# Moving one projection pair ahead of v's stage, sending v's summed weights in one unit of two, and giving the last head one unit less before its products

## The chip, the cores and the metric

The kernel runs on one core of a Trainium2 chip. The metric is device time in microseconds (us) of one execution; the runs shown are three executions of the same program. A profile was taken of a further execution. Its records name the engines PE (TensorE, matmul), PEld (TensorE's load of the stationary operand), DVE (VectorE), ACT (ScalarE), POOL (GpSimd) and SP (the engine that starts most loads). A q behind a name is that engine's sequencer, which issues DMAs.

## What is computed

One decoder layer with two parallel groups, for 512 tokens of width 2048, in float32:

```
h = rmsnorm(x) * g_pre
q, k, v, z_att, u, g_glu, z_conv = split(h @ w_in)          # seven blocks of 1024 columns
# group A: 8 heads of 128, strictly causal stick-breaking attention
z     = q @ k.T / sqrt(128)
log_a = log_sigmoid(z) + (sum of -softplus(z) over the later keys before the query)
y_att = (where(causal, exp(log_a), 0) @ v) * silu(z_att)
# group B: gated, causal depthwise convolution of 31 taps, layer norm, swish, pointwise product
c      = layernorm(conv31(u * sigmoid(g_glu)) + conv_b)
y_conv = (silu(c) @ w_pw2 + b_pw2) * silu(z_conv)
out = x + rmsnorm(concat(y_att, y_conv) @ w_out) * g_post
```

## The kernel before

Every product is made of three matmuls: each operand is split into a rounded upper part (ScalarE, line 104) and the remainder (VectorE, line 105), and hi*hi, lo*hi and hi*lo are accumulated in PSUM (lines 351 to 353; in v's stage 661 to 663). A weight block of 1 MB is loaded by SP into one of two buffers `raw`, split into one of two `hi` and one of two `lo` buffers, and then used.

The work after the input norm is a list of **steps**. A step has one weight block and two **units**; a unit is the matmuls of one PSUM tile, 24 in a projection pair, 12 in v's stage. A `pair` makes 256 columns of a projection in two steps (the two halves of the 2048 rows). The steps are, in order: u pair 0 (`conv_in(0)`), q and k of heads 0 and 1 (`heads(0)`), a g pair (`gate_in(2)`), v's stage (`values()`, seven products `V_ORDER` of two steps each, a scheme with seven instead of eight block products), u pair 1 (`conv_in(1)`), heads 2 and 3, and so on through the other u, q, k and g pairs to the z_att pairs; behind them come z_conv, the pointwise product and the output product. `n_v` and `n_att` are the numbers of v's first step and of the first step behind v's stage, 8 and 22; `n_norm` is 48.

TensorE's order is the order written in the program. The order on VectorE, ScalarE and GpSimd is chosen at compile time by a list scheduler that goes by priorities; each engine then works through its own queue in order. The main loop over the steps (it starts near line 1427) issues beside each unit:

- **v's sums.** Four of v's seven products use weights that are sums of two blocks of `w_in`. The sums are made in device memory by GpSimd's DMA queue, a plain copy (line 528) and an accumulating copy (line 524) per block, 1 MB each, sixteen in all; tiles `vs`. Six are sent during the norm, the other ten one at a time by `sum_next(v_sumq)`, each not before the last matmul of the unit at hand. Products 5, 6, 7 and 4 of `V_ORDER = (1, 2, 5, 6, 3, 7, 4)` use them.
- **the other sums** (`sumq`, tiles `zs` and `ws`), from step 20 on, three in two steps.
- **attention.** `attention()` is a generator, advanced once per unit (`ticks` counts the units). It takes a head when its q and k are there and v's stage is over (`2 * n_att + 1`). For each head it issues the score products (`z`), lets four units pass (`SOFTMAX_TICKS`), issues the transposition of the weights (`aT`, line 742) and their split into `ah` and `al`, lets two units pass (`SPLIT_TICKS`), and issues the products with v (`o_ps`). During the four units ScalarE, VectorE and GpSimd make the weights; GpSimd masks them (line 698). Counted in units, heads 0 to 5 start at 45, 51, 57, 63, 69 and 75, heads 6 and 7 at 84 and 90; head 7's `aT` is at 94 and its `o_ps` at 96, the last unit before `n_norm`.
- **the convolution in the background.** Behind each u pair's second half, `post_u` multiplies the PSUM tile by the gate into `hg` (line 402; its 30 leading zeros are a GpSimd memset, line 401, and there are two `hg` buffers) and queues 32 entries per channel tile: 31 taps on VectorE (lines 405 and 410, tile `acc`) and one addition on GpSimd (line 424 or 426, `ln_sum`). `background` takes four entries after each unit, but one per unit in v's stage, and there the entry is tied behind the newest split of v's weights (`weights_split`). Its entries have a lower priority (`LATER`).

In v's stage VectorE also makes the sums of activations that the seven products need (`make_v_form`, lines 579 to 585) and their splits, and finishes v (`v_done`).

```
            if units_done % 4:
                sum_next(v_sumq)
...
                if n_v <= n < n_att:
                    background(1, LATER, weights_split[0])
                else:
                    background(4, LATER)
```

Of the kernel before, what the change touches and what calls it, by code (L numbers as in the profile page):

```python
# [23 lines left out]
NH = 8  # L24
# [16 lines left out]
SOFTMAX_TICKS, SPLIT_TICKS = 4, 2  # L41
# [12 lines left out]
def hybrid_layer(  # L54
# [127 lines left out]
    def turn_vectors():  # L182
        ps = mm("vec_ps")
        for c in range(CT):
            nc.tensor.transpose(
                ps[:, c * NV : (c + 1) * NV], rows[c // 4][:, c % 4 * P : (c % 4 + 1) * P],
                ident[:NV, :NV],
            )
        nc.vector.tensor_copy(
            vec, ps[:, : CT * NV].rearrange("p (c v) -> p c v", v=NV)  # L190
        )
# [166 lines left out]
    def pair(c0, post, name):  # L358

        ps = {}  # L360

        def unit(half, i):
            def go(w):
                hi, lo = w
                if half == 0:
                    ps[i] = mm(f"{name}_{i}")
                cs = slice(i * P, (i + 1) * P)
                for n in range(8):

                    k = n if c0 != C_U else (n + 4) % 8  # L370
                    mm3(
                        ps[i], (hi[:, k, cs], lo[:, k, cs]), h_at(half * 8 + k),
                        half == 0 and n == 0, half == 1 and n == 7,
                    )
                if half == 1:
                    post(i, ps[i])
            return go

        for half in range(2):
            src = w_in[half * 1024 : (half + 1) * 1024, c0 : c0 + 256]  # L380
            steps.append(Step(
                lambda src=src, half=half: stream(src, 8, f"{name}{half}"),
                [unit(half, 0), unit(half, 1)],
            ))
# [6 lines left out]
    def post_g(c):  # L391
        def post(i, ps):
            sig[c + i] = t2(f"sig{c + i}")
            nc.scalar.activation(sig[c + i], ps, AF.Sigmoid)
        return post

    def post_u(c):
        def post(i, ps):
            ct = c + i
            hg = hgp.tile([P, TAPS - 1 + S], F32, tag="hg", name=f"hg{ct}")  # L400
            nc.gpsimd.memset(hg[:, : TAPS - 1], 0.0)
            nc.vector.tensor_tensor(out=hg[:, TAPS - 1 :], in0=ps, in1=sig.pop(ct), op=ALU.mult)
            acc = t2(f"acc{ct}")
            conv[ct] = acc
            bgq.append(lambda: nc.vector.tensor_scalar(
                out=acc, in0=hg[:, 0:S], scalar1=vec[:, ct, 0:1],
                scalar2=vec[:, ct, V_CB : V_CB + 1], op0=ALU.mult, op1=ALU.add,
            ))
            for j in range(1, TAPS):
                bgq.append(lambda j=j: nc.vector.scalar_tensor_tensor(  # L410
                    out=acc, in0=hg[:, j : j + S], scalar=vec[:, ct, j : j + 1], in1=acc,
                    op0=ALU.mult, op1=ALU.add,
                ))
            bgq.append(lambda: add_to_sum(ct))
        return post
# [21 lines left out]
    def layer_norm():  # L437

        mu = mean_of(ln_sums[0], "mu")
        yield  # L440
        sqs = [late(f"ln_sq{c}") for c in range(CT)]
        for c in range(CT):
            nc.vector.tensor_tensor(out=conv[c], in0=conv[c], in1=mu, op=ALU.subtract)
            nc.scalar.activation(sqs[c], conv[c], AF.Square)
            if c >= 2:
                eng = nc.gpsimd if c % 2 == 0 else nc.vector
                eng.tensor_tensor(out=sqs[c % 2], in0=sqs[c % 2], in1=sqs[c], op=ALU.add)
            yield
        nc.vector.tensor_tensor(out=sqs[0], in0=sqs[0], in1=sqs[1], op=ALU.add)
        var = mean_of(sqs[0], "var")  # L450
        v, y, t = late("ln_v"), late("ln_y"), late("ln_t")
        nc.vector.tensor_scalar_add(v, var, LN_EPS)
        tc.keep_in_program_order(nc.scalar.preload_act_table_set(LN_EXP))
        rsqrt(y, v, t)
        yield
        for c in range(CT):
            nc.vector.tensor_tensor(out=conv[c], in0=conv[c], in1=y, op=ALU.mult)
            nc.scalar.activation(
                conv[c], conv[c], AF.Silu, scale=vec[:, c, V_LG : V_LG + 1],
                bias=vec[:, c, V_LB : V_LB + 1],  # L460
            )
            yield
        for c in range(CT):
            s_hi[c], s_lo[c] = late(f"s_hi{c}", F32R), t2(f"s_lo{c}", F32R)
            split(s_hi[c], s_lo[c], conv[c])
            yield
# [69 lines left out]
    def sum_next(todo):  # L536

        if todo:
            tc.add_manual_dep(
                todo.popleft()().ins, latest[0].name,  # L540
                mybir.DependencyInfo(mybir.DependencyClass.Sync, mybir.DependencyReason.DATA),
                reason="not before its step",
            )
# [127 lines left out]
    def values():  # L671
        for q in V_ORDER:
            for kg in range(2):
                steps.append(Step(
                    lambda q=q, kg=kg: v_load(q, kg), [v_unit(q, kg, 0), v_unit(q, kg, 1)]
                ))
# [80 lines left out]
    def attention():  # L757

        while True:
            while not heads_ready or ticks[0] < max(heads_ready[0][1], 2 * n_att + 1):  # L760
                yield
            h = heads_ready.popleft()[0]
            stages = attend(h)
            for wait in (SOFTMAX_TICKS, SPLIT_TICKS, 0):
                next(stages)
                for _ in range(wait):
                    yield
# [199 lines left out]
    def load_final():  # L967
        for e in range(4):
            gp[e] = fin.tile([P, S], F32, tag="gp", bufs=4, name=f"gp{e}")
            nc.sync.dma_start(gp[e], g_post[e * S : (e + 1) * S].partition_broadcast(P))  # L970
# [212 lines left out]
    def heads(t):  # L1183
        pair(C_Q + t * 256, post_q(2 * t), f"q{t}")
        pair(C_K + t * 256, post_k(2 * t), f"k{t}")
# [4 lines left out]
    def gate_in(t):  # L1190
        pair(C_G + t * 256, post_g(2 * t), f"g{t}")

    def conv_in(t):
        pair(C_U + t * 256, post_u(2 * t), f"u{t}")

    conv_in(0)
    heads(0)
    gate_in(2)
    n_v = len(steps)
    values()  # L1200
    n_att = len(steps)
    conv_in(1)
    heads(1)
    conv_in(2)
    heads(2)
# [199 lines left out]
    units_done, due = 0, 0  # L1405
    for n, step in enumerate(steps):
        if n == n_att:
            start.close()
            zp = att.enter_context(tc.tile_pool(name="zp", bufs=1, space=bass.MemoryType.PSUM))
            op = att.enter_context(tc.tile_pool(name="op", bufs=1, space=bass.MemoryType.PSUM))  # L1410
            attp = att.enter_context(tc.tile_pool(name="attp", bufs=1))
        if n == n_norm:
            att.close()
            conv_stack.close()
            op2 = ctx.enter_context(
                tc.tile_pool(name="op2", bufs=4, space=bass.MemoryType.PSUM)
            )
            late_stack = ExitStack()
            late_pool = late_stack.enter_context(tc.tile_pool(name="late", bufs=11))
            ln = layer_norm()  # L1420
            bgq.extend([lambda: next(ln, None)] * (3 * CT + 3))
        if n == n_pw - 1:
            make_form(ORDER[0])
        if n == n_pw:
            late_stack.close()
            fin = ctx.enter_context(tc.tile_pool(name="fin", bufs=1))
            load_final()
        if SUMS_FROM <= n < n_zc - 1 or n >= n_in:
            due += SUMS_A_STEP
        if n + 1 < len(steps) and n + 1 not in loaded:  # L1430
            loaded[n + 1] = steps[n + 1].load()
        w = loaded.pop(n)
        for unit in step.units:
            unit(w)
            units_done += 1
            if units_done % 4:
                sum_next(v_sumq)
            if due >= 1:
                sum_next(sumq)
                due -= 1  # L1440
            if n == 0 and unit is step.units[0]:
                turn_vectors()
            if n < n_norm:
                ticks[0] += 1
                next(heads_run)
# [5 lines that stand above are left out]
                background(2, LATER)  # L1451
# [28 lines left out]
```

## Time and profile before

| | |
|---|---|
| median of the three runs | 857.69 us |
| the three runs | 857.68, 857.69, 864.57 us |
| the profiled execution | 858.71 us |
| its span, first to last instruction | 857.0 us |
| granted TensorE clock, mean | 0.998 |
| TensorE busy | 847.6 us (99%), 3872 matmuls |
| VectorE, ScalarE, GpSimd busy | 658.5, 417.3, 137.6 us |
| moved by DMA | 195.04 MB |

The profile page lists busy times by engine, then groups of instructions by line; further views give, for one stretch of time, the instructions of an engine in order, with the idle time before each and what ended it, or the busy time of all engines. In a row such as "116.73 0.39 PE L352 MATMUL k<-h_lo,h_k" the first number is the start in us from the start of the span and the second the length. A matmul's length includes its way through the array, so lengths overlap, and the distance of starts is the rate. "<-" in brackets names what ended the wait.

By TensorE's timeline, u pair 0 starts at 61.2 us, q at 83.9, k at 105.6, g at 128.8, v's stage at 150.5, u pair 1 at 227.2, and the second q at 250.9; the last `o_ps` starts at 548.1.

### The profile page before, as it was taken

The page shows a single profiled execution, that of the slowest core. Times are in us where ns is not written, and L with a number is a line of the kernel's source. Part 1 is how long each engine was busy: PE and PEld are TensorE (multiplying, and loading weights), DVE is VectorE, ACT ScalarE, POOL GpSimd, SP SyncE. Part 2 cuts the span into 40 slices and gives each one's busy share as a digit, 9 for nine tenths or more (in the row PEclk, how much of TensorE's full clock was granted, in tenths as well). Part 3 has the DMA queues.
Part 4 walks back from the last instruction along what each step waited for, and adds up shares of the span by engine and source line. Part 5 has one row for each costly group of instructions (what it writes and reads, how often), then busy time and mean ns, then how long its engine had stood idle before and what let it go on. Part 6 is the DMA issues. An engine that isn't in the chain of part 4 may idle for free.

```text
span 857.0 us, 9935 instructions
## 1 busy us (share of the span) xinstructions
PE 847.6 (99%) x3872; PEld 702.3 (82%) x3872; DVE 658.5 (77%) x791; ACT 417.3 (49%) x475; POOL 137.6 (16%) x170
## 2 busy tenths in 40 slices
PE   9999999999999999999999999999999999999996
PEld 7888878888888888888888888888888888888885
DVE  5698899777589798997969898468964776458774
ACT  6784222565534342436432535369843356455543
POOL 0111110010130223222121333330000100000031
PEclk9999999999999999999999999999999999999999
DMA  8798989575877879876689887937755995557783
GB/s 317 243 289 196 325 256 234 191 225 196 299 229 209 245 148 215 276 197 196 191 222 188 235 245 159 283 103 289 295 197 197 220 263 205 197 197 260 288 282 102
DMA packets 92278, 195.04 MB, mean 228 GB/s; under 512 B 3702, under 2 KB 46210, under 8 KB 86856
## 3 DMA queue, kind: packets, MB, share of 16 engines
q1 hardware_dynamic: 66688, 120.74, 41.0%
q0 software_dynamic: 22304, 69.21, 33.7%
q10 hardware_dynamic: 3240, 4.46, 1.5%
q8 instruction: 30, 0.49, 0.2%
q14 instruction: 16, 0.13, 0.0%
HBM read 186.01 MB, written 75.50 MB: 305 GB/s over the span
## 4 chain that ended last, share of the span: by engine, by line
PE 91%; DMA 4%; DVE 2%; ACT 2%; issue 0%; POOL 0%; ACTq 0%; DVEq 0%; POOLq 0%
PE za L351 3%; PE za L353 3%; PE a L1089 3%; PE za L352 3%; PE a L1090 3%; PE a L1091 3%; PE k L353 3%; PE k L351 3%; PE k L352 3%; PE u L351 3%; PE u L353 3%; PE u L352 3%; PE q L353 3%; PE q L351 3%; PE q L352 3%; DMA r_q<-in_w_in_dram 2%
## 5 line engine op out<-in xcount | busy, mean ns | idle before, releaser
L410 DVE SCALAR_TENSOR_TENSOR acc<-hg,vec,acc 128x512 f32<-128x512 f32 x240 | 183.1, 763 | 7.2
L105 DVE TENSOR_TENSOR l_w<-r_w,h_w 128x2048 fp32r<-128x2048 f32 x28 | 64.2, 2292 | 43.5 <-ACT h_w L104 43.5
L104 ACT ACTIVATE h_w<-r_w 128x2048 fp32r<-128x2048 f32 x28 | 53.6, 1916 | 43.4 <-DMA r_w<-ws 16.9
L353 PE MATMUL k<-h_hi,l_k 128*128 128x512 f32 x128 | 50.0, 390 | 1.1 <-DVE l_k L105 1.1
L351 PE MATMUL u<-h_hi,h_u 128*128 128x512 f32 x128 | 50.1, 392 | 0.0
L351 PE MATMUL q<-h_hi,h_q 128*128 128x512 f32 x128 | 50.1, 392 | 0.0
L351 PE MATMUL za<-h_hi,h_za 128*128 128x512 f32 x128 | 50.1, 391 | 0.0
L351 PE MATMUL k<-h_hi,h_k 128*128 128x512 f32 x128 | 50.1, 391 | 0.0
L353 PE MATMUL q<-h_hi,l_q 128*128 128x512 f32 x128 | 49.9, 390 | 0.0
L353 PE MATMUL za<-h_hi,l_za 128*128 128x512 f32 x128 | 49.9, 390 | 0.0
L353 PE MATMUL u<-h_hi,l_u 128*128 128x512 f32 x128 | 49.9, 390 | 0.0
L352 PE MATMUL u<-h_lo,h_u 128*128 128x512 f32 x128 | 49.8, 389 | 0.0
L352 PE MATMUL za<-h_lo,h_za 128*128 128x512 f32 x128 | 49.8, 389 | 0.0
L352 PE MATMUL q<-h_lo,h_q 128*128 128x512 f32 x128 | 49.8, 389 | 0.0
L352 PE MATMUL k<-h_lo,h_k 128*128 128x512 f32 x128 | 49.8, 389 | 0.0
L1091 PE MATMUL a<-h_w,f_lo 128*128 128x512 f32 x128 | 49.8, 389 | 0.0
L1089 PE MATMUL a<-h_w,f_hi 128*128 128x512 f32 x128 | 49.8, 389 | 0.0
L1090 PE MATMUL a<-l_w,f_hi 128*128 128x512 f32 x128 | 49.8, 389 | 0.0
L105 DVE TENSOR_TENSOR l_z<-r_z,h_z 128x2048 fp32r<-128x2048 f32 x14 | 32.1, 2291 | 16.3 <-ACT h_z L104 16.3
L105 DVE TENSOR_TENSOR l_v<-r_v,h_v 128x2048 fp32r<-128x2048 f32 x14 | 32.1, 2290 | 15.3 <-ACT h_v L104 15.3
L698 POOL TENSOR_SCALAR_AFFINE_SELECT t<-t 128x128 f32<-128x128 f32 x64 | 33.6, 562 | 54.1 <-ACT t L734 30.1
L104 ACT ACTIVATE h_v<-r_v 128x2048 fp32r<-128x2048 f32 x14 | 26.8, 1916 | 29.6 <-PE g L352 13.2
(381 smaller groups left out, 2238.2 us busy)
## 6 DMA issues: line engine op xcount, KB each, us to landing
ws<-in_w_out_dram POOLq DMA_DIRECT2D x24, 1024.0 KB, 9.4
r_w<-ws SPq DMA_DIRECT2D x16, 1024.0 KB
vs<-in_w_in_dram POOLq DMA_DIRECT2D x12, 1024.0 KB, 12.7
zs<-in_w_in_dram POOLq DMA_DIRECT2D x12, 1024.0 KB, 9.3
r_w<-in_w_out_dram SPq DMA_DIRECT2D x12, 1024.0 KB
r_u<-in_w_in_dram SPq DMA_DIRECT2D x8, 1024.0 KB
r_q<-in_w_in_dram SPq DMA_DIRECT2D x8, 1024.0 KB
r_k<-in_w_in_dram SPq DMA_DIRECT2D x8, 1024.0 KB
```

What stands on the lines that cost most here:

```text
L104: nc.scalar.activation(hi, src, AF.Copy)
L105: made = nc.vector.tensor_tensor(out=lo, in0=src, in1=f32(hi), op=ALU.subtract)
L351: nc.tensor.matmul(ps, wh, ah, start=first, stop=False)
L352: nc.tensor.matmul(ps, wh, al, start=False, stop=False)
L353: latest[0] = nc.tensor.matmul(ps, wl, ah, start=False, stop=last).ins
L410: bgq.append(lambda j=j: nc.vector.scalar_tensor_tensor(out=acc, in0=hg[:, j : j + S], scalar=vec[:, ct, j : j + 1], in1=acc, op0=ALU.mult ...
L698: nc.gpsimd.affine_select(out=blk, in_=blk, compare_op=ALU.is_gt, fill=0.0, base=0, pattern=[[-1, P]], channel_multiplier=1,)
L1089: nc.tensor.matmul(ps, fh[:, kk, ts], hi[:, k, :], start=st, stop=False, skip_group_check=True)
L1090: nc.tensor.matmul(ps, fh[:, kk, ts], lo[:, k, :], start=False, stop=False, skip_group_check=True)
L1091: nc.tensor.matmul(ps, fl[:, kk, ts], hi[:, k, :], start=False, stop=en, skip_group_check=True)
```

## The change

Three edits:

1. `conv_in(1)`, the second u pair, stands in front of v's stage instead of behind it. `n_v` becomes 10 and `n_att` 24; from step 24 on the steps have their old numbers. Attention's first head starts at unit 49 instead of 45.
2. One of v's sums is sent after every second unit (units 1, 3, 5 and so on) instead of after three units of four.
3. For the last head one unit instead of two passes between the transposition and the products. Its `aT` is at unit 95 and its `o_ps` at 96.

```diff
             stages = attend(h)
-            for wait in (SOFTMAX_TICKS, SPLIT_TICKS, 0):
+
+            for wait in (SOFTMAX_TICKS, SPLIT_TICKS if h < NH - 1 else SPLIT_TICKS - 1, 0):
                 next(stages)
...
     heads(0)
     gate_in(2)
+    conv_in(1)
     n_v = len(steps)
     values()
     n_att = len(steps)
-    conv_in(1)
     heads(1)
...
             units_done += 1
-            if units_done % 4:
+            if units_done % 2:
                 sum_next(v_sumq)
```

## The prediction, made before the changed kernel had run

> **What bounds the kernel now.** I read the page's head first, then who TensorE waited for, then TensorE's own timeline.
>
> ```profile
> span 857.0 us, 9935 instructions
> PE 847.6 (99%) x3872; PEld 702.3 (82%) x3872; DVE 658.5 (77%) x791; ACT 417.3 (49%) x475; POOL 137.6 (16%) x170
> ```
>
> TensorE is busy 847.6 of 857.0 us, so it is the bound, and what a change can win is what TensorE waits. A busy matmul in these records may still hide a late start, so the spacing of starts is the better witness. The next two views are TensorE's waits and its timeline around the longest one (start, length, line, idle before and releaser).
>
> ```profile
> PE idle L1283 <- POOL mean_w L140: 1.8, 1, 1.8
> PE last L1159 <- ACT diag L1158: 1.5, 1, 1.5
> PE k L353 <- DVE l_k L105: 1.1, 1, 1.1
> 116.50 0.39 PE L351 MATMUL k<-h_hi,h_k 128*128 128x512 f32 x1
> 116.73 0.39 PE L352 MATMUL k<-h_lo,h_k 128*128 128x512 f32 x1
> 118.20 0.50 PE L353 MATMUL k<-h_hi,l_k 128*128 128x512 f32 x1 [1.08 <-DVE l_k L105]
> 194.13 0.39 PE L661 MATMUL vb<-h_v,vf_00h 128*128 128x512 f32 x1
> 194.51 0.50 PE L662 MATMUL vb<-l_v,vf_00h 128*128 128x512 f32 x1
> ```
>
> Full-width matmuls start 0.23 us apart (116.50 to 116.73). Of TensorE's three waits two stand at the first and the last products, which the diff leaves alone. The third is k's second half: 118.20 - 116.73 - 0.23 = **1.24 us** lost. Inside v's stage 194.13 to 194.51 loses 0.15 us. Apart from those and the fixed start and end there is nothing on TensorE to win.
>
> [...]
>
> **Why k is late.** The chain of waits in order of time, then GpSimd's queue over the same stretch.
>
> ```profile
> 70.78 19.23 DMA r_q<-in_w_in_dram
> 94.84 18.96 DMA r_k<-in_w_in_dram
> ...
> 67.15 1.18 POOL L524 DMA_DIRECT2D vs<-in_w_in_dram  x1 [6.01 <-PE u L353]
> 73.45 1.16 POOL L524 DMA_DIRECT2D vs<-in_w_in_dram  x1 [5.12 <-PE u L353]
> 78.89 0.75 POOL L528 DMA_DIRECT2D vs<-in_w_in_dram  x1 [4.28 <-PE u L353]
> 89.77 0.73 POOL L528 DMA_DIRECT2D vs<-in_w_in_dram  x1 [10.13 <-PE q L353]
> 95.21 1.18 POOL L524 DMA_DIRECT2D vs<-in_w_in_dram  x1 [4.71 <-PE q L353]
> 100.65 1.17 POOL L524 DMA_DIRECT2D vs<-in_w_in_dram  x1 [4.25 <-PE q L353]
> ```
>
> One weight block of 1 MB takes 19 us to land, twice in a row, while a step of two units (48 matmuls 0.23 apart) lasts 11 us. Beside these two loads GpSimd sends six transfers of v's sums, 1 MB each, three units out of four. The fourth-unit pause is the hole between 78.89 and 89.77.
>
> **The change, part by part.**
>
> *One unit in two.* Ten sums are left when the steps begin. They now go after units 1, 3, 5 up to 19 instead of 1, 2, 3, 5 up to 13. Between 67 and 101 us four are sent (about 67, 78, 89, 100) where six were. During r_k's landing, from 94.84 for 18.96 us, the accumulating ones of 95.21 and 100.65 become one plain copy at 100. r_q's load likewise loses one of three neighbours. If the loads share the traffic evenly, a load beside two sums that falls to one goes from a third of the bandwidth to a half: 18.96 x 2/3 = 12.6 us, 6 us sooner, against 1.24 us needed. So the whole stall goes: **-1.24 us**; the bounds are 0 (the load is slow for another reason) and -1.24 (nothing more was lost there). What is late next is the step itself: q's second half has no measurable loss. The last sum is now sent after unit 19, in the second u pair; v's first product from a sum comes at the fifth v step, ten units later, so nothing waits for it.
>
> [...]
>
> *The u pair moved.* Its 96 matmuls, two 1 MB loads, their splits, two multiplications and two GpSimd memsets stay the same, so TensorE's sum is unchanged. SP's queue takes the two loads in the same step order as TensorE. What moves is the vector work: 62 convolution taps and two sums follow this pair in the queue of background work. Before, 8 entries were left for v's 28 units, which take one each; now 56 are left, and 28 run beside v. That is 20 more entries.
>
> ```profile
> 150.00:226.00 76.00, 76.00 (x335) 62.30 (x334) 56.26 (x51) 41.86 (x42) 4.47 (x4) 1.00 0.62 210
> 94.72 8.62 DVE L410 SCALAR_TENSOR_TENSOR acc<-hg,vec,acc 128x512 f32<-128x512 f32 x11
> 154.84 1.54 DVE L410 SCALAR_TENSOR_TENSOR acc<-hg,vec,acc 128x512 f32<-128x512 f32 x2
> 158.13 2.29 DVE L105 TENSOR_TENSOR l_v<-r_v,h_v 128x2048 fp32r<-128x2048 f32 x1 [1.75 <-ACT h_v L104]
> 161.65 0.39 PE L662 MATMUL vc<-l_v,h_hi 128*128 128x512 f32 x1
> 169.48 0.75 DVE L410 SCALAR_TENSOR_TENSOR acc<-hg,vec,acc 128x512 f32<-128x512 f32 x1
> 170.15 2.28 DVE L105 TENSOR_TENSOR l_v<-r_v,h_v 128x2048 fp32r<-128x2048 f32 x1
> 172.53 0.45 PE L662 MATMUL vb<-l_v,vf_00h 128*128 128x512 f32 x1
> 192.16 2.29 DVE L105 TENSOR_TENSOR l_v<-r_v,h_v 128x2048 fp32r<-128x2048 f32 x1 [1.87 <-ACT h_v L104]
> 197.38 2.29 DVE L105 TENSOR_TENSOR l_v<-r_v,h_v 128x2048 fp32r<-128x2048 f32 x1
> ```
>
> A tap costs 8.62 / 11 = 0.78 us, so 20 add 15.7 us to VectorE's 56.3 of 76.0 (first row: window, TensorE, weight loads, VectorE): 72.0 of 76, 95%. It fits, but hardly. Each tap is tied behind the lower part l_v of the newest weights, and the pair at 154.84 shows where that puts it: right after a split, in the hole of 1.75 us before the next one. There two taps (1.54 us) cost nothing. The cover is gone where the forms of the activations crowd VectorE. The split of 170.15 came straight after a tap, ended at 172.43 and was used at 172.53, with 0.1 us to spare. The split of 192.16 ended 0.08 us after TensorE was due to use it (194.13 + 0.23 = 194.36), and that of 197.38 ended at 199.67 for a use due about 199.8. Those last two had no taps near them; now they will. Bounds: -0.15 us (buffers come free in a luckier order and today's loss goes) and two taps before every split, priced below as a rival. I take the nearest row, one tap ahead of one of these two splits: 170.15 - 169.48 = **+0.67 us**. A tap before both costs it only once, as TensorE's delay at the first is margin at the second.
>
> *Attention and its tail.* Attention starts one unit after v's stage in both kernels; the u pair that stood in that place is gone, so, counted in units, heads 0 to 5 come four units later and heads 6 and 7 one unit later. The same instructions run, with fewer taps beside them. Only the last head loses time: its transposed weights get one unit instead of two between their transposition and their products.
>
> ```profile
> 536.07 1.25 PE L742 MATMUL aT<-ident,t 128*128 128x128 f32 x10
> 537.86 1.23 ACT L104 ACTIVATE ah<-aT 128x1280 fp32r<-128x1280 f32 x1
> 540.20 1.48 DVE L105 TENSOR_TENSOR al<-aT,ah 128x1280 fp32r<-128x1280 f32 x1
> 548.10 0.39 PE L351 MATMUL o_ps<-ah,v_hi 128*128 128x512 f32 x1
> ```
>
> From 536.07 the split was done at 541.68, 5.6 us, of 12.0 us given. One unit less (24 matmuls, 5.5 us) leaves 6.5 us, 0.9 us to spare: **0**. Without that cover it would cost what the split is late; the bound from above is one more weight split ahead of it, 2.3 - 0.9 = 1.4 us, from below 0.
>
> *GpSimd's end of v.* The other sums (zs, ws) start at step 20, which is now v's last four steps instead of two and the u pair.
>
> ```profile
> 227.19 0.39 PE L351 MATMUL u<-h_hi,h_u 128*128 128x512 f32 x1
> 219.40 0.77 POOL L528 DMA_DIRECT2D zs<-in_w_in_dram  x1 [30.26 <-PE va L663]
> 224.93 0.73 POOL L528 DMA_DIRECT2D ws<-in_w_out_dram  x1 [4.76 <-PE va L663]
> 227.88 1.92 ACT L104 ACTIVATE h_u<-r_u 128x2048 fp32r<-128x2048 f32 x1 [2.55 <-DMA r_u<-in_w_in_dram]
> ```
>
> Beside two such sums a load reached ScalarE 227.88 - 227.19 = 0.7 us after v's last step had freed its buffer (the u pair starts there). A v step gives its split about 1.2 us to spare (160.42 against a use at 161.65), so I take 0, between 0 and +1.3 (a load late by twice as much).
>
> **Sum.** -1.24 + 0.67 + 0 + 0 = -0.57 us. The profiled execution took 858.71 us, 1.71 around its span, so it would be 858.14. The runs' median, 857.69, lies 1.02 below that execution, and the forecast for a median is **857.1 us**. About 1%, 8.6 us, is what a measurement of this kernel can tell from no change.
>
> **Rivals.**
> 1. *VectorE becomes v's bound* (slower). Its place is the in-order queue of VectorE: two taps stand ahead of the splits instead of behind. At 1.54 us against 1.2 to spare, every second split stalls TensorE by 0.34 (the next one gains that margin): 7 x 0.34 = 2.4, and the two crowded places 1.5 each, 5.4 in all, less 1.24: 861.9. It decides from the second tap ahead of a crowded split, when the loss passes 1.24. For it: 95%. Against it: the tie behind l_v, and 154.84.
> 2. *GpSimd holds up head 0.* GpSimd's memset for the third u pair waits for the taps of the second, which now lie closer to head 0's masks. One such memset has already held the queue:
>
> ```profile
> 175.01 0.12 POOL L401 MEMSET hg<- 128x30 f32 x1 [39.16 <-DVE acc L410]
> 248.60 3.10 POOL L698 TENSOR_SCALAR_AFFINE_SELECT t<-t 128x128 f32<-128x128 f32 x4 [1.50 <-ACT t L734]
> 256.32 1.25 PE L742 MATMUL aT<-ident,t 128*128 128x128 f32 x10
> ```
>
> The masks ended at 251.7 and head 0's transposition began at 256.3, so 4.6 us are free. A hold of 8 us, an estimate of a fifth of that 39.16, would cost 3.4: 857.1 + 3.4 = 860.5.
> 3. *The stall stays* because the loads are slow by themselves: 857.69 + 0.67 = 858.4.
> 4. *No loss in v*, or the old 0.15 goes too: 857.69 - 1.24 = 856.45, or 856.3.
>
> **Chances.** Forecast 0.42, rival 4 0.16, rival 3 0.10, rival 2 0.12, rival 1 0.15 with its tail, and 0.05 for several at once beyond 1%. The range reaches from rival 4 less 0.3 us for another chip, 856.0, to rival 2's 860.5; rival 1 and the last case, 2 in 10, lie outside. Faster by over 1% is closed by TensorE's starts (0.01), slower by over 1% needs more than rival 1 (0.05), the rest is within 1%.
>
> **What would show it.** k's wait for l_k gone from TensorE's waits and r_k landing in under 14 us (step one); l_v waits at vb or va of 0.5 to 1 us in all (step two); o_ps after the last aT without a gap (step three). Many short l_v waits would show rival 1, a wait of aT for t rival 2. I am wrong if TensorE's starts in v show more than 1.2 us lost or the k wait stays.

## The result: slower by 0.7%, and the profile after

The changed kernel takes 864.97 us (median of 14 runs, 863.0 to 867.3) against 857.59 us (14 runs). The ratio of the means is 1.0073, with a 95% interval of 1.0053 to 1.0094: slower, and outside the range of 856.0 to 860.5. Of the 14 runs of the kernel before, 11 lie between 857.0 and 858.6 us and three between 861.5 and 864.8; two profiles of such longer executions, at the end of the experiments, show why.

The profiled execution took 864.89 us with a span of 863.2, 6.2 us longer than before. The head of its page:

```profile
span 863.2 us, 9933 instructions
PE 849.9 (98%) x3872; PEld 703.4 (81%) x3872; DVE 658.0 (76%) x791; ACT 417.1 (48%) x475; POOL 142.8 (17%) x170
```

And TensorE's waits (total, times, longest), without the two at the first and the last products, which are as before:

```profile
PE va L661 <- ACT v_a L621: 1.7, 1, 1.7
PE q L353 <- DVE l_q L105: 1.6, 1, 1.6
PE q L351 <- ACT h_q L104: 1.0, 1, 1.0
PE u L351 <- DVE k_lo L105: 0.5, 1, 0.5
```

The wait of k for l_k is gone, as forecast: k now starts at 105.71 and the g pair behind it at 127.47, 21.76 us for 96 matmuls of 0.227. The split of k's second half on ScalarE, before and after:

```profile
113.90 1.92 ACT L104 ACTIVATE h_k<-r_k 128x2048 fp32r<-128x2048 f32 x1 [11.94 <-DMA r_k<-in_w_in_dram]
105.73 1.92 ACT L104 ACTIVATE h_k<-r_k 128x2048 fp32r<-128x2048 f32 x1 [4.66 <-PE q L352]
```

Four new waits stand in its place, and three of them lie together, at the end of v's stage. TensorE's timeline there:

```profile
238.83 0.39 PE L663 MATMUL va<-h_v,h_lo 128*128 128x512 f32 x1
240.88 0.50 PE L661 MATMUL va<-h_v,h_hi 128*128 128x512 f32 x1 [1.66 <-ACT v_a L621]
...
248.95 0.39 PE L663 MATMUL va<-h_v,h_lo 128*128 128x512 f32 x1
250.36 0.50 PE L351 MATMUL q<-h_hi,h_q 128*128 128x512 f32 x1 [1.03 <-ACT h_q L104]
250.70 0.40 PE L352 MATMUL q<-h_lo,h_q 128*128 128x512 f32 x1
252.69 0.79 PE L353 MATMUL q<-h_hi,l_q 128*128 128x512 f32 x1 [1.59 <-DVE l_q L105]
253.28 0.63 PE L351 MATMUL q<-h_hi,h_q 128*128 128x512 f32 x1
253.71 0.63 PE L352 MATMUL q<-h_lo,h_q 128*128 128x512 f32 x1
```

By the distance of starts less 0.227, 1.82 us are lost at 240.88, 1.18 at 250.36 and 1.76 at 252.69. Behind them matmuls start 0.43 apart, not 0.23. The view by windows (window, TensorE's busy time and matmuls, granted clock, DMA share, GB/s) names the reason:

```profile
250.00:252.00 2.00, 0.73 (x2) 1.00 1.07 199
252.00:254.00 2.00, 1.31 (x3) 0.66 1.10 194
254.00:256.00 2.00, 2.00 (x6) 0.50 1.10 268
256.00:258.00 2.00, 2.00 (x10) 0.99 1.02 393
```

The granted clock fell to half for about 3.4 us, which costs eight matmuls another 1.67 us (3.49 us from 252.69 to 256.18, less eight times 0.227). What made the loads late is seen on GpSimd's queue first:

```profile
228.65 0.76 POOL L528 DMA_DIRECT2D zs<-in_w_in_dram  x1 [61.38 <-PE va L663]
234.09 0.73 POOL L528 DMA_DIRECT2D ws<-in_w_out_dram  x1 [4.68 <-PE va L663]
236.80 0.70 POOL L528 DMA_DIRECT2D zs<-in_w_in_dram  x1 [1.98 <-PE va L663]
239.52 0.70 POOL L528 DMA_DIRECT2D ws<-in_w_out_dram  x1 [2.02 <-PE va L663]
246.92 1.18 POOL L524 DMA_DIRECT2D zs<-in_w_in_dram  x1 [5.34 <-PE va L663]
```

On ScalarE's timeline:

```profile
238.44 1.91 ACT L104 ACTIVATE h_v<-r_v 128x2048 fp32r<-128x2048 f32 x1 [1.78 <-DMA r_v<-vs]
240.26 0.57 ACT L621 COPY v_a<-va 128x512 f32<-128x512 f32 x1
248.40 1.91 ACT L104 ACTIVATE h_q<-r_q 128x2048 fp32r<-128x2048 f32 x1 [3.45 <-DMA r_q<-in_w_in_dram]
```

And in the chain of waits in order of time:

```profile
235.42 12.87 DMA r_q<-in_w_in_dram
```

From 228.65 on the other sums (zs, ws) run beside v's last loads and q's first. ScalarE waits 1.78 us for a load; the copy of v_a queues behind that split, and TensorE needs the copy before it can fill the PSUM bank of va again. Then r_q takes 12.87 us to land and q's split is late.

The ledger of the two profiles: -1.24 (k) - 0.26 (the two late starts behind 194.13, 0.15 and 0.11, which are gone) + 1.82 + 1.18 + 1.76 + 1.67 (clock) + 0.58 (the wait for k_lo, in a u pair at 412.49) + 0.7 in gaps of 0.1 to 0.3, most of them behind waits, = +6.2 us, the difference of the spans.

### The profile page after: what moved, and what is told of

The parts are those of the page before. It is cut to its first block, busy times and chain, and to the rows that moved or that the text cites. A ratio compares the mean times of both kernels' runs of the same rounds, so it can differ in the third digit from the quotient of the medians.

```text
span 863.2 us, 9933 instructions
## 1 busy us (share of the span) xinstructions
PE 849.9 (98%) x3872; PEld 703.4 (81%) x3872; DVE 658.0 (76%) x791; ACT 417.1 (48%) x475; POOL 142.8 (17%) x170
## 4 chain that ended last, share of the span: by engine, by line
PE 85%; DVE 8%; ACT 3%; DMA 2%; issue 1%; POOL 0%; DVEq 0%; ACTq 0%; POOLq 0%
PE q L353 3%; PE q L351 3%; PE q L352 3%; PE a L1091 3%; PE a L1092 3%; PE a L1090 3%; PE za L351 3%; PE za L353 3%; PE za L352 3%; PE u L351 3%; PE k L351 3%; PE k L353 3%; PE u L352 3%; PE k L352 3%; PE u L353 3%; DVE acc L410 2%
## 5 line engine op out<-in xcount | busy, mean ns | idle before, releaser
L410 DVE SCALAR_TENSOR_TENSOR acc<-hg,vec,acc 128x512 f32<-128x512 f32 x240 | 180.1, 750 | 6.6
L698 POOL TENSOR_SCALAR_AFFINE_SELECT t<-t 128x128 f32<-128x128 f32 x64 | 36.0, 596 | 74.2 <-DVE t L721 46.0
```

What stands on the lines that cost most here:

```text
L410: bgq.append(lambda j=j: nc.vector.scalar_tensor_tensor(out=acc, in0=hg[:, j : j + S], scalar=vec[:, ct, j : j + 1], in1=acc, op0=ALU.mult ...
L698: nc.gpsimd.affine_select(out=blk, in_=blk, compare_op=ALU.is_gt, fill=0.0, base=0, pattern=[[-1, P]], channel_multiplier=1,)
```

## Experiments

Theory D: the other sums start at a step number (20), and v's stage has slid under it by two steps. Their transfers now meet loads for steps that last 5.4 us, where before they met loads for the u pair's steps of 10.9 us. Theory V is the forecast's first rival, VectorE overfull with taps. The kernel before took 857.28 us beside the first four experiments below, 857.36 beside the next four and 857.59 beside the last four; each ratio is to those runs.

**The loss without the moved pair.** The kernel before, with the sums two steps sooner:

```diff
-SUMS_FROM, SUMS_A_STEP = 20, 1.5
+SUMS_FROM, SUMS_A_STEP = 18, 1.5
```

> The kernel before (second u pair behind v, no more taps beside v) with the other sums started at step 18 instead of 20, so that they meet v's last four steps as in the changed kernel. Theory D: the loss appears without the moved pair, TensorE waits at v's last product or the pair behind it, 860 to 866 us. Theory V: 857 to 858 us, as before.

864.53 us, ratio 1.0084 (1.0069 to 1.0099). TensorE's new waits in this kernel:

```profile
PE u L353 <- DVE l_u L105: 1.6, 1, 1.6
PE u L351 <- ACT h_u L104: 1.5, 1, 1.5
```

The same pair of waits stands at the pair behind v, here u, and the matmuls behind it start 0.43 apart. The sums' place against v makes the whole loss; neither the u pair nor its taps are needed for it.

**No taps beside v.** The changed kernel with

```diff
-                    background(1, LATER, weights_split[0])
+                    background(0, LATER, weights_split[0])
```

> The changed kernel without any background entry beside v's stage; the 56 taps and sums left there run later, four per unit. Theory D: the sums still collide with the loads, 863 to 866 us. Theory V: VectorE has room again, 856 to 858 us.

865.31 us, ratio 1.0089 (1.0074 to 1.0104): the loss is all there. Theory V falls.

**The sums behind v, or two steps later.** The changed kernel with SUMS_FROM at 24 and at 22:

> The changed kernel, with the other sums (zs, ws) started at step 24, behind v's stage, instead of step 20. Theory D (these sums now share the transfers with v's last loads and the first loads behind v, so TensorE waits there and its clock falls): the waits at va and q between 240 and 257 us go, and the time is 856 to 857.5 us, below the kernel before. Theory V (the 20 more taps beside v make VectorE the bound): nothing changes, about 865 us.

> The changed kernel, with the other sums started at step 22, which is v's last product, where they stood beside v in the kernel before. Theory D: v's last product starts undisturbed and the loads behind it are short of bandwidth for one product instead of two, so most of the loss goes: 856.5 to 859 us. Theory V: about 865 us.

871.26 us (1.0165, 1.0148 to 1.0182) and 870.27 us (1.0150, 1.0135 to 1.0165): both theories missed. No wait is left at va or q in either, so D was right about the place. The loss went to the output product, where TensorE waits longest. Its waits there, with the sums from 24:

```profile
PE a L1090 <- ACT h_w L104: 8.3, 1, 8.3
PE a L1091 <- DVE l_w L105: 1.5, 1, 1.5
```

GpSimd's queue ahead of them:

```profile
696.28 3.57 POOL L524 DMA_DIRECT2D ws<-in_w_out_dram  x3 [0.30 <-issue]
```

And ScalarE:

```profile
717.85 1.91 ACT L104 ACTIVATE h_w<-r_w 128x2048 fp32r<-128x2048 f32 x1 [13.81 <-DMA r_w<-in_w_out_dram]
```

With the same rate from a later start, sums are left over when the output product begins. There the matmul that a sum has to wait for is no longer renewed, so the last ones leave together (696.28) and the next weights land late. The sums are a debt that must be paid before the output product.

**The sums behind v, faster.** The changed kernel with

```diff
-SUMS_FROM, SUMS_A_STEP = 20, 1.5
+SUMS_FROM, SUMS_A_STEP = 24, 1.75
```

> The changed kernel with the other sums started at step 24 and 1.75 instead of 1.5 of them per step, so that as many are done by the gates' stage as in the kernel before. Theory D: neither v's end nor the output product waits, 856 to 857 us. Rival (1.75 MB of sums per step is more than the loads behind v can bear): the loss comes back as several waits between 250 and 550 us, 858 to 865 us.

857.97 us, ratio 1.0000 (0.9986 to 1.0014). The whole loss is gone, and its 12 runs lie between 857.63 and 858.84. It is no gain on the kernel before: by the medians it is 0.6 us slower, and of the new waits only the one for k_lo, 0.58 us, is left. One window over v's stage (window, TensorE, weight loads, VectorE, ScalarE, GpSimd busy, clock, DMA share, GB/s), first of the changed kernel:

```profile
171.00:250.00 79.00, 76.68 (x337) 62.73 (x335) 66.69 (x70) 40.61 (x40) 5.80 (x8) 1.00 0.72 247
```

And of this one:

```profile
171.00:250.00 79.00, 79.00 (x350) 65.12 (x349) 71.51 (x76) 43.78 (x43) 1.80 (x2) 1.00 0.62 204
```

VectorE is busy 71.51 of 79 us, 91%, and TensorE doesn't wait once in v. What fell is the transfers, from 247 to 204 GB/s, and with them the time of a load. The first load for q is started at 235.6 here, and its split begins at 242.28 without waiting for it:

```profile
242.28 1.92 ACT L104 ACTIVATE h_q<-r_q 128x2048 fp32r<-128x2048 f32 x1
```

So it took at most 6.7 us, where the same load, started at 235.42, took 12.87 in the changed kernel.

**The same six sums, spread thinly over v.**

```diff
-SUMS_FROM, SUMS_A_STEP = 20, 1.5
+SUMS_FROM, SUMS_A_STEP = 12, 1.5
...
-            due += SUMS_A_STEP
+            due += SUMS_A_STEP if n >= n_att else 0.5
```

> The changed kernel with the other sums spread thinly over v's stage: half a sum per step from step 12 to 23, six in all as in the changed kernel, then 1.5 per step. Theory D: a single sum beside a load does not make it late, so no wait at v's end and none at the output product: 856 to 857 us. Rival (any such sum beside v's loads costs TensorE time): six waits of 0.5 to 1 us in v, 859 to 863 us.

863.36 us, ratio 1.0071 (1.0044 to 1.0098); the rival held, with three waits in v and one at q instead of six in v. The three longest:

```profile
PE q L353 <- DVE l_q L105: 1.6, 1, 1.6
PE va L662 <- DVE l_v L105: 1.4, 1, 1.4
PE va L661 <- ACT v_a L621: 0.5, 1, 0.5
```

ScalarE's timeline at v's end:

```profile
234.12 1.92 ACT L104 ACTIVATE h_v<-r_v 128x2048 fp32r<-128x2048 f32 x1 [3.19 <-DMA r_v<-vs]
248.44 1.92 ACT L104 ACTIVATE h_q<-r_q 128x2048 fp32r<-128x2048 f32 x1 [3.41 <-DMA r_q<-in_w_in_dram]
```

Even with one sum in two steps ScalarE stands 3.2 and 3.4 us waiting for loads. The clock stayed up here (mean 0.999), so the waits alone make this loss.

**One edit alone: one unit in two.** The kernel before with `units_done % 2`.

> The kernel before with one edit of the change: v's sums after one unit in two. Theory D (one unit in two takes away the 1.24 us stall of k, and all of the loss comes from where the other sums meet v's end): 856.0 to 856.5 us against 857.3, k's wait gone. Rival (the wait of k is only moved to a later step by the sums that now go later): 857.3 us, with a new wait in g's or v's first steps.

864.54 us, ratio 1.0071 (1.0047 to 1.0095); the rival held, and harder than it said. GpSimd's last two of v's sums:

```profile
152.15 1.19 POOL L524 DMA_DIRECT2D vs<-in_w_in_dram  x1 [7.66 <-PE va L663]
157.59 1.16 POOL L524 DMA_DIRECT2D vs<-in_w_in_dram  x1 [4.25 <-PE va L663]
```

The split behind them on ScalarE:

```profile
165.67 1.91 ACT L104 ACTIVATE h_v<-r_v 128x2048 fp32r<-128x2048 f32 x1 [7.76 <-DMA r_v<-in_w_in_dram]
```

And TensorE's waits:

```profile
PE vc L661 <- ACT h_v L104: 2.2, 1, 2.2
PE vc L662 <- DVE l_v L105: 1.8, 1, 1.8
```

Behind them the 13 matmuls from 170.55 to 175.67 start 0.43 apart, and the mean clock of this execution is 0.994. Here v's own sums run into v's first steps, and it is D's mechanism once more. In the changed kernel the u pair's 21.8 us take them in.

**One edit alone: the last head.**

> The kernel before with one edit of the change: the last head's products one unit sooner. Theory D: no loss, 857.3 us within 0.3, no gap at the last head's products. Rival (one unit is too short for the split of the transposed weights): a wait of TensorE there of 0.5 us or more.

857.16 us, ratio 0.9988 (0.9972 to 1.0003), and no wait at the last head's products: this edit costs nothing.

**One unit in two undone in the changed kernel.**

> The changed kernel with v's sums again after three units of four; the u pair stays ahead of v. Theory D: v's sums are done before v in both, so the loss at v's end stays, 864 to 866 us; k may wait 0 to 1.2 us more. Rival (the late end of v's sums is what costs, as in the kernel with that edit alone): 857 to 859 us.

869.06 us (865.88 to 873.57), ratio 1.0123 (1.0077 to 1.0169). The loss at v's end stays, as D says, but 4 us more than in the changed kernel were not expected. The intervals of the two ratios overlap, and the profile is of the fastest of its four runs. In it k waits 0.99 and 1.76 us, so the slower sending is worth something in front of v; where the other runs lose more is not shown.

**Work added into the wait.** Are the slow matmuls a price of their own? In front of the first q behind v, 13 products that wait for no load:

```diff
+                if (c0, half, i) == (C_Q + 256, 0, 0):
+                    for _ in range(13):
+                        nc.tensor.matmul(ps[i], mean_w, h_at(0)[0], start=True, stop=True)
                 for n in range(8):
```

> The changed kernel with 13 more full-width products, written to q's PSUM tile before its own first product overwrites them, in front of the first q behind v, where TensorE waits. They are 13 x 0.227 = 2.95 us of extra work and take no data that is waited for. Theory C (the slow matmuls behind the two waits are a clock lowered because TensorE stood nearly idle, and cost 2.4 us of their own): the fillers lie in the wait, the matmuls behind start 0.227 apart, and the time falls by 2 to 2.5 us to 862.5. Rival (the slow matmuls have another cause, say late weights): the time stays at 865 or grows by up to 2.9 us.

863.70 us (12 runs), ratio 1.0065 (1.0046 to 1.0083), against the changed kernel's 864.97 and 1.0073. With 2.95 us more work the kernel is not slower; the medians say 1.3 us faster, half of what was expected, but the two were not run side by side and the intervals overlap. TensorE's timeline:

```profile
248.87 3.19 PE L370 MATMUL q<-h_hi,mean_w 128*128 128x512 f32 x13
251.90 0.40 PE L351 MATMUL q<-h_hi,h_q 128*128 128x512 f32 x1
252.13 0.40 PE L352 MATMUL q<-h_lo,h_q 128*128 128x512 f32 x1
```

And the clock behind it, by windows:

```profile
252.00:254.00 2.00, 2.00 (x11) 1.00 1.08 157
```

With TensorE kept at work the clock stayed at 1.00 and the products behind start 0.23 apart. The slow products of the changed kernel were thus a matter of the clock, lowered by TensorE's waits, and not of late weights.

**The kernel before, twice more.** Unchanged, for its profile.

> The kernel before once more, unchanged in what it does, for a second profile. Theory S (k's wait of 1.24 us in the first profile belonged to that execution and not to the kernel): no wait at k or one well under 1 us. Rival (it is there each time): 1 to 1.3 us.

> The same again, a third profile of the kernel before. Theory S: no wait at k or one well under 1 us. Rival: 1 to 1.3 us.

These two executions took 861.47 and 863.62 us, and both theories were wrong: the wait is neither absent nor constant. In the first, q waited 0.39 and 1.76 us and k 0.99; in the second, by the chain:

```profile
70.87 24.26 DMA r_q<-in_w_in_dram
```

and by TensorE's waits:

```profile
PE q L351 <- ACT h_q L104: 2.7, 1, 2.7
PE q L353 <- DVE l_q L105: 1.6, 1, 1.6
```

r_q took 24.26 us to land in this execution and 19.23 in the first profile. Behind the waits matmuls start 0.43 apart here too. In the two kernels that share the steps up to k with the kernel before (the sums from 18, the last head alone), the profiles show no wait at q or k at all. The loads in front of v are thus a race that most executions win and some lose by 4 to 7 us.

## Why the prediction was wrong

1. *What bounds the kernel*: right. TensorE's starts carry all of the difference, in the ledger above.
2. *One unit in two, -1.24 us*: the mechanism was right, the size was that of one execution. The loads do land sooner: k's second split starts between 105.41 and 105.90 us in all eight profiles with this edit, and between 111.05 and 116.41 in all six without it. But the profiled execution lay 1.02 us above the median, and the wait was most of that distance. The prediction took off both, and so counted most of that time twice. For the median the edit was worth about nothing in front of v: the profiled execution of the last head alone, without this edit, has no wait at k and took 857.15 us. What the edit can save are the lost races; that it saves all of them is not shown.
3. *The u pair moved, +0.67 us by taps*: wrong. In the changed kernel no matmul of v waits for an l_v, and the 0.26 us behind 194.13 are gone; with the sums behind v and faster, 91% of VectorE was reached without a wait. The first rival falls with it.
4. *Attention and its tail, 0*: right for the last head. Missed: 0.58 us at a u pair, whose bank waits for k_lo behind four taps, in all seven profiles with the moved pair and with taps beside v, and not in the one without those taps.
5. *GpSimd's end of v, 0 with +1.3 as the upper end*: **the step that failed.** It measured 1.82 + 1.18 + 1.76 us of waits and 1.67 us of lowered clock, 6.4 us. The prediction saw that the sums now start two steps deeper in v. It priced them by the one load that was 0.7 us late beside two sums, a load for a step of 10.9 us, and didn't ask how much lateness a step of 5.4 us bears when several loads in turn are late. The upper end was no better founded: 1.3 is neither twice 0.7 nor what is left of it after the 1.2 us to spare. It also left out the clock, which stood at half for 3.4 us behind waits of 1.18 and 1.76 us.
6. *The rivals*: the slower one named the right stage and the wrong resource. It was VectorE's queue that looked full, at 95% by the estimate; the transfers, at 0.62 of the DMA engines, looked free. Rivals 2 and 3 did not come: in the changed kernel no aT waits for t, and k's wait is gone.

## What to carry to other kernels

When a stage is moved, look for everything that is scheduled by a step number and ask what it now lies beside; here a background stream of transfers kept its number while the stage slid under it. A stage with short steps and double buffers may bear little other traffic, even where its mean DMA share leaves room (here v's stage had 0.62 without these sums, and one sum in two steps already cost 6 us), and transfers that are put off come due later. A profile is one execution: where its time lies off the median, find which wait makes the difference before giving that wait a price.

## What the runs showed of the hardware

In the changed kernel TensorE waited 1.18 and 1.76 us with two matmuls between, and the granted clock then stood at half for 3.4 us, which adds 1.67 us to the ledger above. In the kernel before with the sums from 18 it stood at half for about 6.8 us, by the windows behind the two waits at u (window, TensorE's busy time and matmuls, granted clock, DMA share, GB/s):

```profile
228.00:230.00 2.00, 0.41 (x3) 0.65 1.10 200
230.00:232.00 2.00, 2.00 (x5) 0.50 1.13 209
232.00:234.00 2.00, 2.00 (x6) 0.50 1.10 288
234.00:236.00 2.00, 2.00 (x8) 0.64 1.04 408
```

Not every such wait did this. In the execution with edit 2 undone k waits 0.99 and 1.76 us, and v's end has a single wait of 2.03 us:

```profile
116.00:118.00 2.00, 1.17 (x5) 1.00 0.09 29
118.00:120.00 2.00, 0.41 (x2) 1.00 0.42 147
120.00:122.00 2.00, 2.00 (x10) 1.00 0.60 177
242.00:244.00 2.00, 0.18 (x1) 1.00 1.09 396
244.00:246.00 2.00, 2.00 (x8) 0.76 1.06 423
246.00:248.00 2.00, 2.00 (x6) 0.50 1.02 416
248.00:250.00 2.00, 2.00 (x9) 0.88 1.01 374
```

A window less its busy time is its idle time. The two waits at k left TensorE idle for 2.42 us between 116 and 120, and the clock stayed at 1.00. The single wait left it idle for 1.82 us between 242 and 244, and the clock then stood at half for about 3.4 us. So neither the length of a wait nor the idle time of two together decides in this execution; what does is not shown. These idle times go by the matmuls' ends in the trace, which are modelled.

In the changed kernel matmuls start 0.43 us apart where the granted clock is 0.50, and 0.23 apart where it is 1.00.

A second surprise is how much a load's landing varies in one and the same program: r_q took 19.23 us in one execution of the kernel before and 24.26 in another.
